# A two-layer decoder step: the last LayerNorm's mean subtracted in PSUM, its channel sums folded, some running sums added by DMA

## The chip, the core and the metric

The kernel runs on one core of a Trainium2 chip. The metric is the device time of one execution in microseconds; before the change the median of three runs is 2298.3 us (2297.39 to 2299.56). Engines are called TensorE (PE in the profile), VectorE (DVE), ScalarE (ACT), GpSimd (POOL) and SyncE (SP, which issues most DMAs). SBUF is the on-chip memory of 128 partitions, PSUM the small memory with 2 KB banks into which TensorE accumulates.

## What is computed

One step of a decoder with two layers, over 1024 prompt tokens and 8 decode tokens, model width D = 2048, all in 32-bit floats. Only the frame matters here:

```python
def layer_norm(x, g, b):                 # over the 2048 channels of a token
    mu = jnp.mean(x, -1); var = jnp.mean((x - mu)**2, -1)
    return (x - mu) * rsqrt(var + 1e-5) * g + b

z = x @ w_in                             # layer A: pooling mixer
y = (mix(z) * silu(gate)) @ w_out
h = layer_norm(ALPHA * x + y, g, b)
k, v = shared_kv(h)                      # once
z = h @ w_in                             # layer B: sliding-window attention
y = (attention(z, k, v) * silu(gate)) @ w_out
out = layer_norm(ALPHA * h + y, g, b)    # the last norm; prompt and decode tokens
```

## The kernel before

**Layout.** Channels lie on the 128 partitions, tokens along the free axis. The 2048 channels are 16 tiles of 128, kept as 8 **pairs** p = 0..7 (tiles 2p and 2p+1, side by side in one buffer). The 1032 tokens are two **chunks**: chunk 0 has 512, chunk 1 has 520 (512 and the 8 decode tokens). Chunk 1 is worked on in two **halves** of 260 tokens, `HV[0]` and `HV[1]`. A norm over channels is therefore a sum over partitions, which TensorE forms by a product with a matrix J that holds 1/2048 everywhere; J lies in `cst` as plain fp32 and in `jr` as fp32r, a form that TensorE multiplies faster with a rounded operand.

**Matmuls.** Each fp32 weight and activation is split into a rounded high part and a low part; a product is three fp32r matmuls, high x high, high x low and low x high (L594 to L596). ScalarE makes the high part (`cast`, L386), VectorE the low one (`low`, L394). The four big products, in order `ai`, `ao` (layer A, in and out) and `bi`, `bo` (layer B), use a seven-product scheme over 2x2 blocks, in three groups: A (products 0 and 5), C (1, 3, 6) and B (2, 4).

**Units and the calendar.** `plan` writes the work of TensorE out as a list of units; one unit is 25 matmuls of 260 columns, some 3 us. The clock `self.i` counts units. `on(t, f)`, `at(n, f)` and `product(n, f)` fix f at the end of a unit; `soft` puts a task with a due time into a list, from which `gentle` takes what a rough model of each engine's load allows; generators in `self.side` (the norms) are stepped when the model sees calm, or after `every` units at the latest. `in_order` then fixes the order of PE, DVE and ACT to that of the source. SP and POOL are issued in the order that the framework's own scheduler finds. SBUF is 53 slots of 1040 columns (`Mem`), each taken whole or as two half slots; a freed slot is given out again oldest first.

**The end of the kernel.** Group B of `bo` makes the output of chunk 1. Product 2 of position pos gives tiles of pair pos//2 + 4, product 4 those of pair pos//2. Positions 0 to 3 run over all 520 tokens; so pairs 4, 0, 5, 1 are finished first, in this order. Then come 16 units for positions 4 to 7, eight on the first half of the tokens and eight on the second, which finish pairs 6, 2, 7, 3. A bank for product 2 is first filled with what earlier products left (`recall`, a ScalarE copy at L716, two units ahead), and what is done is added to it in PSUM; the VectorE addition at L665 (`post`) takes product 4 out of PSUM into SBUF.

The last norm of chunk 1 goes along in pieces:
- `tail_full` is called for pairs 4, 0, 5, 1. For pair 4 it takes a rough mean by TensorE and subtracts it (`rough`, `mean`, `less`, L1187 to L1201); later units have it subtracted in PSUM (L603). For each pair it then squares (ScalarE, L1205) and adds value and square to two running sums (VectorE, `add`, L1211 and L1212, 1040 columns each).
- `tail_part` does the same for pairs 6, 2, 7 per half: `square` (L1235), `add` (L1239, L1240, 520 columns). For pair 3 it calls `tail_sums`.
- `tail_sums` (L1269) sums over partitions with plain fp32 J: running value and running square of both tiles, and value and square of pair 3, into two banks. An fp32 product stands in the trace as two instructions; over one half that is 2 banks x 4 sources x 2 = 16.
- `tail_stats` (L1281 to L1283) copies the mean, squares it, forms the variance; `rstd` (L849 to L853) makes the inverse deviation by ScalarE's reciprocal square root and one Newton step on VectorE.
- `tail_norm` for each pair: subtract the mean (`tail_less`, L1288, VectorE), multiply by the inverse deviation (L1295, VectorE, 520 columns), gain and bias for both tiles (L1299, ScalarE), and the output DMA (L1300, 260 KB). For the first half these steps run beside the units of the second half.
- `tail_end`, after the last unit, does the same for the second half, pairs in the order 4, 0, 5, 2, 1, 6, 7, 3.

The norm of chunk 0 is `ln_gen`, a generator; its two channel sums, of values and of squares, are formed one after the other by `j_gen` (L828 to L845: fold the pair, split in high and low, two matmuls with `jr`). `ao` has the same norm for its own output.

## Time and profile before

| | |
|---|---|
| median of three runs | 2298.3 us (2297.39 to 2299.56) |
| the profiled execution's own time | 2300.38 us |
| its span, first to last instruction or transfer | 2298.6 us |
| its mean granted clock of TensorE | 0.995 |
| instructions | 42483 |
| matmul instructions of TensorE | 17158 |
| `cast` L386 | 365, 1045 ns each |
| `low` L394 | 365, 1219 ns each |

How to read the rows that the prediction quotes. Engine lines of the page give busy us, share of the span and instruction count. A timeline row is: start in us from the span's start, duration (of a whole group, if several), engine, line, operation, output<-input, partitions x elements, count, and in brackets the wait just before it with the instruction that ended it. A row of waits is: engine, output, line <- releasing engine, output, line: total us, count, longest. A row of windows is: stretch, its length, then busy us and instruction count of PE, PEld, DVE, ACT and POOL, then TensorE's granted clock (1 is full speed), the DMA engines' busy share and GB/s. A row of output DMAs gives the issuing queue, the KB moved and the first and last start. "x16" is a count of instructions; "m" is a slot in SBUF, "pD" or "pO" a bank of PSUM.

### The profile page before, as it was taken

To read this page: it belongs to the slowest core of one execution; us is meant where nothing else is said; L and a number is where in the kernel's file an instruction comes from. 1 tells how busy PE (TensorE), PEld (TensorE's weight loads), DVE (VectorE), ACT (ScalarE), POOL (GpSimd) and SP (SyncE) were. 2 spreads that over 40 slices of the span, in tenths; PEclk is the share of its full clock that TensorE was granted. 3 is DMA by queue.
4 is the path that set the end of the run, shared out by engine and by line. 5 is a ranking of instruction groups with operands and counts; after the bars stand their busy time and mean duration, and the time that the engine had idled before them with its cause. 6 is when DMAs were issued, how large, how long until landed. Compare 5 with 4: busy or idle time off the path is not lost.

```text
span 2298.6 us, 42483 instructions
## 1 busy us (share of the span) xinstructions
PE 2266.7 (99%) x17158; PEld 2124.4 (92%) x17158; DVE 1577.5 (69%) x1958; ACT 1119.2 (49%) x2321; POOL 195.4 (8%) x415
## 2 busy tenths in 40 slices
PE   8999999999999999999999999999999999999996
PEld 7888999999999899998788899999999998889996
DVE  6547656746577587666786867666667778687677
ACT  5243333344334443445576644545557777443355
POOL 1101001100101011000011101010000000111000
PEclk9999999999999999999999999999999999999998
DMA  9958667673757798888497776666744566898853
GB/s 377 311 192 294 210 221 243 235 249 117 246 179 273 266 337 296 297 272 302 150 313 266 258 252 206 214 220 201 245 146 135 176 204 221 256 375 298 296 192 130
DMA packets 194645, 555.68 MB, mean 242 GB/s; under 512 B 31120, under 2 KB 36112, under 8 KB 194448
## 3 DMA queue, kind: packets, MB, share of 16 engines
q1 hardware_dynamic: 152752, 402.42, 53.9%
q0 software_dynamic: 41696, 150.55, 16.9%
q8 instruction: 134, 2.20, 0.4%
q14 instruction: 63, 0.52, 0.1%
HBM read 372.04 MB, written 171.33 MB: 236 GB/s over the span
## 4 chain that ended last, share of the span: by engine, by line
PE 92%; DVE 4%; DMA 2%; ACT 1%; issue 1%; SPq 0%; ACTq 0%; DVEq 0%
PE pD L594 27%; PE pD L595 27%; PE pD L596 27%; PE pD L1056 4%; PE pO L1574 2%; PE pS L1492 2%; PE pS L1545 1%; DMA m<-in_wob 1%; DVE m L1295 0%; DMA to<-m 0%; DVE m L1288 0%; DMA m<-to 0%; DVE m L394 0%; DVE m L926 0%; PE pD L1269 0%
## 5 line engine op out<-in xcount | busy, mean ns | idle before, releaser
L594 PE MATMUL pD<-m,m 128*128 128x260 f32 (+1 forms) x4800 | 1456.2, 303 | 9.4 <-ACT m L1836 5.8
L595 PE MATMUL pD<-m,m 128*128 128x260 f32 (+1 forms) x4800 | 1447.5, 302 | 0.2 <-DVE m L527 0.2
L596 PE MATMUL pD<-m,m 128*128 128x260 f32 (+1 forms) x4800 | 1447.6, 302 | 0.0
L594 PEld LDWEIGHTS pD<-m,m 128*128 128x128 f32 x4800 | 905.3, 189 | 52.4 <-ACT m L1836 5.8
L595 PEld LDWEIGHTS pD<-m,m 128*128 128x128 f32 x4800 | 905.2, 189 | 36.3 <-DVE m L527 1.2
L596 PEld LDWEIGHTS pD<-m,m 128*128 128x128 f32 x4800 | 904.8, 189 | 35.6
L394 DVE TENSOR_TENSOR m<-m,m 128x1024 fp32r<-128x1024 f32 x365 | 443.5, 1219 | 166.1 <-ACT m L386 148.1
L386 ACT CAST m<-m 128x1024 fp32r<-128x1024 f32 x365 | 380.1, 1045 | 40.7 <-PE pD L595 9.6
L430 DVE TENSOR_TENSOR m<-m,m 128x1024 f32<-128x1024 f32 x200 | 244.0, 1220 | 21.6 <-DMA m<-in_woa 6.0
L654 ACT COPY m<-pD 128x260 f32<-128x260 f32 (+1 forms) x126 | 55.9, 444 | 313.4 <-PE pD L596 297.0
L527 DVE TENSOR_TENSOR m<-m,m 128x1040 fp32r<-128x1040 f32 x111 | 133.6, 1235 | 21.3 <-ACT m L521 21.1
L521 ACT CAST m<-m 128x1040 fp32r<-128x1040 f32 x111 | 114.0, 1061 | 33.6 <-DMA m<-h 9.1
L663 ACT ACTIVATE m<-pD 128x260 f32<-128x260 f32 x100 | 38.6, 386 | 180.5 <-PE pD L596 167.2
L665 DVE TENSOR_TENSOR m<-pD,m 128x260 f32<-128x260 f32 x100 | 42.5, 425 | 109.8 <-PE pD L596 103.4
L1527 ACT ACTIVATE m<-m,sm 128x128 f32<-128x128 f32 x256 | 99.3, 393 | 0.0
L1056 PE MATMUL pD<-m,m 128*128 128x260 f32 (+1 forms) x576 | 91.4, 319 | 0.0
L1056 PEld LDWEIGHTS pD<-m,m 128*128 128x128 f32 x576 | 82.0, 188 | 8.3
L1557 DVE TENSOR_TENSOR m<-m,cst 128x1024 f32<-128x1024 f32 x32 | 39.1, 1222 | 73.1 <-ACT m L1553 73.1
L1540 ACT ACTIVATE m<-m,sm 128x128 f32<-128x128 f32 x256 | 81.8, 395 | 9.6 <-DVE sm L1535 9.6
L620 ACT ACTIVATE m<-pD 128x512 f32<-128x512 f32 x50 | 29.8, 596 | 115.8 <-PE pD L596 107.4
L635 ACT COPY m<-pD 128x260 f32<-128x260 f32 x68 | 25.6, 376 | 122.1 <-PE pD L596 122.1
L633 ACT ACTIVATE m<-pD 128x260 f32<-128x260 f32 x68 | 26.4, 388 | 113.5 <-PE pD L596 113.5
(183 smaller groups left out, 1689.6 us busy)
## 6 DMA issues: line engine op xcount, KB each, us to landing
m<-in_wib SPq DMA_DIRECT2D x96, 512.0 KB, 5.3
m<-in_wia SPq DMA_DIRECT2D x95, 512.0 KB, 5.5
m<-in_woa SPq DMA_DIRECT2D x48, 512.0 KB, 6.7
m<-in_wob SPq DMA_DIRECT2D x48, 512.0 KB, 6.9
sbi<-m POOLq DMA_DIRECT2D x36, 512.0 KB, 4.4
m<-sbi SPq DMA_DIRECT2D x36, 512.0 KB, 4.2
m<-in_x SPq DMA_DIRECT2D x35, 520.0 KB, 8.5
sai<-m POOLq DMA_DIRECT2D x32, 512.0 KB, 4.1
```

The costliest lines, as they stand in the source:

```text
L386: self.nc.scalar.copy(e["hi"].r[:, :1024], e["raw"].a[:, :1024])
L394: self.nc.vector.tensor_sub(o.r[:, :1024], s.a[:, :1024], e["hi"].a[:, :1024])
L430: self.nc.vector.tensor_add(s[o].a[:, :1024], s[a].a[:, :1024], s[b].a[:, :1024])
L521: self.nc.scalar.copy(h.r[:, : 2 * TMAX], s.a[:, : 2 * TMAX])
L527: self.nc.vector.tensor_sub(o.r[:, : 2 * TMAX], s.a[:, : 2 * TMAX], h.a[:, : 2 * TMAX])
L594: nc.tensor.matmul(ps[:, :w], wh[:, s], h, start=new and n2 == 0, stop=False, skip_group_check=on)
L595: nc.tensor.matmul(ps[:, :w], wh[:, s], l, start=False, stop=False, skip_group_check=on)
L596: nc.tensor.matmul(ps[:, :w], wl[:, s], h, start=False, stop=n2 == 7, skip_group_check=on)
L654: self.evac(ph, pos)(self.dest(ph, pos, m, 0)(cs), ps[:, : cs.stop - cs.start])
L1056: nc.tensor.matmul(ps[:, : cs.stop - cs.start], ws[:, s], d[:, cs], start=f0 and k == 0, stop=l0 and k == 3,)
L1527: nc.scalar.activation(x["s3"][:, i, :], x["s3"][:, i, :], AF.Exp, bias=nm[:, i : i + 1], scale=0.125, accum_out=rs[:, i : i + 1],)
L1540: nc.scalar.activation(x["s3"][:, i, :], x["s3"][:, i, :], AF.Copy, scale=rs[:, i : i + 1])
```

## The change

What it does, part by part.
- **Two sums at once.** A new `two_gen` takes the place of `j_gen` in the norms of chunk 0: values and squares are folded, split and multiplied with `jr` side by side, into two banks. `ln_gen` yields once more at odd pairs in the last norm, and that norm's pace is set to 1 at unit 7 of the group where it was 2 at unit 13.
- **Casts.** A lone weight's cast may be queued at `min(L_CAST + 2, lead - 2)` units ahead of use; where the load leads by less than the usual 11 units, this is later than before.
- **Running sums.** In `tail_full`, pairs 5 and 1 are added to the running sums by accumulating DMAs on GpSimd's queue (`accum_op=add`, SBUF to SBUF), squares and additions right at the end of the unit. In `tail_part` the same holds for pair 6 (both halves) and pair 2 (first half). The other additions stay on VectorE, one unit earlier but for pair 2 in the second half.
- **Folded sums.** After pair 7, VectorE adds tile 1 of both running sums to tile 0. Pair 3 is folded in too (tile 0 of the second half and both tiles of the first). `tail_sums` then has one source for each bank, and in the second half also the last tile of pair 3.
- **First half earlier.** Its sums stay where they were, statistics and norms come one unit earlier, and the norm of its pair 3 moves into `tail_end`.
- **Mean in PSUM.** The new `tail_end` handles six of eight pairs so: TensorE copies a tile into a bank with the identity matrix in fp32 (`fill`), adds `jr` times the high and low part of -16 x mean (`less`; 128 rows of 1/2048 sum to 1/16), and VectorE multiplies the bank by the inverse deviation. Pairs 4 and 0 keep the subtraction on VectorE. Three tiles of the twelve get gain and bias on VectorE, the others on ScalarE; results go to SBUF or back into the bank.

```diff
         self.on(t - lead, load, 6)
-        self.rounds(t, e)
+        self.rounds(t, e, min(L_CAST + 2, lead - 2))
         return e
...
-    def rounds(self, t, e):
+    def rounds(self, t, e, early=L_CAST + 2):
...
-        e["queue"] = lambda: self.soft("a", t - L_CAST - 2, t - L_CAST + 1, cast_task)
+        e["queue"] = lambda: self.soft("a", t - early, t - L_CAST + 1, cast_task)
...
+    def two_gen(self, T, acc, sq, mu, q, v):
+
+        nc, w = self.nc, []
+        for s in (acc, sq):
+            t = self.pair_view(s, T)
+            nc.vector.tensor_add(t[:, 0], t[:, 0], t[:, 1])
+            e = self.mem.full()
+            w.append((s, t, e, e.r[:, :T], e.r[:, TMAX : TMAX + T]))
+            nc.scalar.copy(w[-1][3], t[:, 0])
+        yield
+        for s, t, e, hi, lo in w:
+            nc.vector.tensor_sub(lo, t[:, 0], hi.bitcast(F32))
+            s.free()
+        yield
+        ps = []
+        for s, t, e, hi, lo in w:
+            ps.append(self.psW()[:, :T])
+            for i, a in enumerate((hi, lo)):
+                nc.tensor.matmul(ps[-1], self.jr, a, start=i == 0, stop=i == 1)
+            e.free()
+        yield
+        nc.scalar.activation(q, ps[0], AF.Square)
+        nc.scalar.copy(mu, ps[0])
+        nc.vector.scalar_tensor_tensor(v, ps[1], EPS, q, op0=ALU.add, op1=ALU.subtract)
+        yield
...
-        yield from self.j_gen(T, acc, lambda s, ps: nc.scalar.copy(mu[:, s], ps))
-        w = self.mem.full()
-        q, v = w.a[:, :T], w.a[:, TMAX : TMAX + T]
         if c == 0:
-            sq = self.l_sq
-            nc.vector.tensor_mul(q, mu, mu)
+            w = self.mem.full()
+            q, v = w.a[:, :T], w.a[:, TMAX : TMAX + T]
+            yield from self.two_gen(T, acc, self.l_sq, mu, q, v)
         else:
+            yield from self.j_gen(T, acc, lambda s, ps: nc.scalar.copy(mu[:, s], ps))
+            w = self.mem.full()
+            q, v = w.a[:, :T], w.a[:, TMAX : TMAX + T]
...
-        yield from self.j_gen(
-            T, sq,
-            lambda s, ps: nc.vector.scalar_tensor_tensor(v[:, s], ps, EPS, q[:, s], op0=ALU.add, op1=ALU.subtract)
-            if c == 0 else nc.vector.tensor_scalar(v[:, s], ps, EPS, None, op0=ALU.add),
-        )
+            yield from self.j_gen(T, sq, lambda s, ps: nc.vector.tensor_scalar(v[:, s], ps, EPS, None, op0=ALU.add))
...
                 if c == 0:
                     nc.vector.tensor_sub(t, t, b2(mu))
+                    if name is None and p % 2:
+                        yield
                 nc.vector.tensor_mul(t, t, b2(rr))
...
             a = self.tacc
-            nc.vector.tensor_add(flat(a), flat(self.tp[4] if q == 0 else a), flat(s))
-            nc.vector.tensor_add(flat(self.tq[4]), flat(self.tq[4]), flat(self.tq[q]))
-            self.tq.pop(q).free()
+            z = self.tq.pop(q)
+            if q == 0:
+                nc.vector.tensor_add(flat(a), flat(self.tp[4]), flat(s))
+                nc.vector.tensor_add(flat(self.tq[4]), flat(self.tq[4]), flat(z))
+                z.free()
+                return
+            nc.gpsimd.dma_start(flat(a), flat(s), accum_op=ALU.add)
+            nc.gpsimd.dma_start(flat(self.tq[4]), flat(z), accum_op=ALU.add)
+            z.free(True)
...
-        for n, go in ((3, square), (4, add)):
+        for n, go in ((3, square), (4, add)) if q in (0, 4) else ((0, square), (0, add)):
             self.at(n, go)
...
+        a, z = self.pair_view(self.tacc, TMAX), self.qv(4)
+
         def add():
-            a, z = self.pair_view(self.tacc, TMAX), self.qv(4)
+            y = self.tq.pop((q, h.start))
+            if q == 6 or q == 2 and not final:
+                nc.gpsimd.dma_start(a[:, :, h], self.tv(q)[:, :, h], accum_op=ALU.add)
+                nc.gpsimd.dma_start(z[:, :, h], y.v(2, THM), accum_op=ALU.add)
+                y.free(True)
+                return
             nc.vector.tensor_add(a[:, :, h], a[:, :, h], self.tv(q)[:, :, h])
-            nc.vector.tensor_add(z[:, :, h], z[:, :, h], self.tq[q, h.start].v(2, THM))
-            self.tq.pop((q, h.start)).free()
-
-        if q == 3 and final:
+            nc.vector.tensor_add(z[:, :, h], z[:, :, h], y.v(2, THM))
+            y.free()
+            if q == 7:
+                for u in (a, z):
+                    nc.vector.tensor_add(u[:, 0, h], u[:, 0, h], u[:, 1, h])
+
+        def fold():
+            nc.vector.tensor_add(a[:, 0, h], a[:, 0, h], self.tv(q)[:, j, h])
+            nc.vector.tensor_add(z[:, 0, h], z[:, 0, h], self.tq[q, h.start].v(2, THM)[:, j])
+
+        if q == 3:
             square(j)
-            self.product(0 if j else 1, lambda: self.tail_sums(h, (j,), j == 0, j == 1), 1)
+            if j and final:
+                self.product(0, lambda: self.tail_sums(h, (1,)), 1)
+                return
+            self.at(0, fold, 6)
+            if j:
+                self.product(1, lambda: self.tail_sums(h, ()), 1)
+                self.at(1, lambda: self.tail_stats(h))
+                for n, p in zip((2, 3, 3, 4, 4, 5, 6), (4, 0, 5, 1, 6, 2, 7)):
+                    self.at(n, lambda p=p: self.tail_norm(p, h))
             return
         if j == 0:
             return
         self.at(0, square)
-        if q != 3:
-            self.at(1, add)
-            return
-        self.product(1, lambda: self.tail_sums(h, (0, 1), True, True), 1)
-        self.at(2, lambda: self.tail_stats(h))
-        for n, p in zip((3, 4, 4, 5, 5, 6, 6, 7), (4, 0, 5, 1, 6, 2, 7, 3)):
-            self.at(n, lambda p=p: self.tail_norm(p, h))
-
-    def tail_sums(self, h, js, first, stop):
+        self.at(1 if q == 2 and final else 0, add, 6)
+
+    def tail_sums(self, h, js):
         J = self.cst[:, K_J : K_J + P]
-        if first:
-            self.R[h.start] = self.psW(), self.psW()
-        for ps, a, z in zip(
-            self.R[h.start], (self.pair_view(self.tacc, TMAX), self.qv(4)),
+        R = self.R[h.start] = self.psW(), self.psW()
+        pairs = list(zip(
+            R, (self.pair_view(self.tacc, TMAX), self.qv(4)),
             (self.tv(3)[:, :, h], self.tq[3, h.start].v(2, THM)),
-        ):
-            srcs = ([a[:, j, h] for j in range(2)] if first else []) + [z[:, j] for j in js]
-            for i, v in enumerate(srcs):
-                self.nc.tensor.matmul(
-                    ps[:, :THM], J, v, start=first and i == 0, stop=stop and i == len(srcs) - 1,
-                    skip_group_check=not (first and stop),
-                )
+        ))
+        for n, j in enumerate((None,) + js):
+            for ps, a, z in pairs:
+                v = a[:, 0, h] if j is None else z[:, j]
+                self.nc.tensor.matmul(ps[:, :THM], J, v, start=n == 0, stop=n == len(js), skip_group_check=True)
...
     def tail_end(self):
-        h = HV[1]
-        self.tail_stats(h, lambda: [self.tail_less(p, h) for p in (4, 0)])
-        for p in (4, 0, 5, 2, 1, 6, 7, 3):
-            self.tail_norm(p, h, p not in (4, 0))
-
+
+        nc, h = self.nc, HV[1]
+        ident = self.cst[:, K_ID : K_ID + P]
+        mb, vb = (b[:, :THM] for b in self.R[h.start])
+        _, r, qq, v = (self.L[k][:, h] for k in "mrqv")
+        sl = self.mem.full()
+        hi, lo = (sl.r[:, i * THM : (i + 1) * THM] for i in range(2))
+        mean = mb[:, None, :].to_broadcast([P, 2, THM])
+        banks = [self.psO(), self.psD(), self.psD(), self.psD(), self.psW(), self.psW()]
+        plain, tiles = (4, 0), [2 * p + j for p in (5, 1, 2, 6, 7, 3) for j in range(2)]
+        done = []
+
+        def z(k):
+            return self.tv(k // 2)[:, k % 2, h]
+
+        def bank(n):
+            if n >= 6:
+                banks.append((self.psO, self.psD, self.psD, self.psD, self.psW, self.psW)[n % 6]())
+            return banks[n][:, :THM]
+
+        def fill(n):
+            nc.tensor.matmul(bank(n), ident, z(tiles[n]), start=True, stop=False, skip_group_check=True)
+
+        def less(n):
+            for i, t in enumerate((hi, lo)):
+                nc.tensor.matmul(banks[n][:, :THM], self.jr, t, start=False, stop=i == 1, skip_group_check=True)
+
+        def scale(k, src, eng):
+            g, b = (self.prm[:, i + k : i + k + 1] for i in (C_GB, C_BB))
+            if eng == "a":
+                nc.scalar.activation(z(k), src, AF.Identity, bias=b, scale=g)
+            else:
+                nc.vector.tensor_scalar(z(k), src, g, b, op0=ALU.mult, op1=ALU.add)
+            done.append(k)
+            if k ^ 1 in done:
+                p = k // 2
+                nc.sync.dma_start(self.io["y1"][:, 2 * p : 2 * p + 2, h], self.tv(p)[:, :, h])
+
+        self.tail_norm(3, HV[0])
+        nc.scalar.activation(qq, mb, AF.Square)
+        nc.scalar.mul(hi, mb, -16.0)
+        nc.vector.scalar_tensor_tensor(v, vb, EPS, qq, op0=ALU.add, op1=ALU.subtract)
+        nc.vector.scalar_tensor_tensor(lo, mb, -16.0, hi.bitcast(F32), op0=ALU.mult, op1=ALU.subtract)
+
+        def between():
+            for p in plain[:1]:
+                t = self.tv(p)[:, :, h]
+                nc.vector.tensor_sub(t, t, mean)
+
+        for n in range(4):
+            fill(n)
+        for n in range(4, 6):
+            less(n - 4)
+            fill(n)
+        less(2)
+        less(3)
+        self.rstd(v, r, qq, between)
+        two = r[:, None, :].to_broadcast([P, 2, THM])
+        for n, k in enumerate(tiles):
+            if n in (1, 4):
+                p = plain[n > 1]
+                t = self.tv(p)[:, :, h]
+                if n > 1:
+                    nc.vector.tensor_sub(t, t, mean)
+                nc.vector.tensor_mul(t, t, two)
+                for j in range(2):
+                    scale(2 * p + j, t[:, j], "a")
+            if n + 4 < len(tiles):
+                less(n + 4)
+            b = banks[n][:, :THM]
+            eng = "v" if n in (7, 9, 11) else "a"
+            o = z(k) if eng == "v" or n + 6 < len(tiles) else b
+            nc.vector.tensor_mul(o, b, r)
+            scale(k, o, eng)
+            if n + 6 < len(tiles):
+                fill(n + 6)
...
-        self.on(f["bo", "B"] + 13, pace(2))
+        self.on(f["bo", "B"] + 7, pace(1))
```

More of the change, by code (lines that the diff above doesn't have):

```diff
@@ L476, in weights @@
                 src = {0: a11, 5: a12, 2: ws[:, 0, :], 4: ws[:, 1, :]}[u.idx]
-                held[k] = self.lone(u.t, src, L_LOAD - (4 if u.keep else 2 if (u.ph, u.grp) == ("bi", "B") else 0))
+                lead = L_LOAD - (4 if u.keep else 2 if (u.ph, u.grp) == ("bi", "B") else 0)
+                held[k] = self.lone(u.t, src, lead)
             u.ent = held[k]
```

## The prediction

> **What bounds the kernel now.** I read the page first, then the waits of TensorE over the whole span, then the timelines of TensorE, VectorE and ScalarE from 2195 us on, where every part of the change that is not a reordering lies.
>
> ```profile
> span 2298.6 us, 42483 instructions
> PE 2266.7 (99%) x17158; PEld 2124.4 (92%) x17158; DVE 1577.5 (69%) x1958; ACT 1119.2 (49%) x2321; POOL 195.4 (8%) x415
> PE 92%; DVE 4%; DMA 2%; ACT 1%; issue 1%; SPq 0%; ACTq 0%; DVEq 0%
> PE pS L1492 <- DVE m L1475: 2.3, 1, 2.3
> PE pD L594 <- DVE m L629: 2.2, 1, 2.2
> PE pD L594 <- ACT m L663: 0.3, 1, 0.3
> PE pD L1269 <- DVE m L1239: 0.5, 1, 0.5
> ```
>
> TensorE is busy 99% of the span, and its waits between the first matmul and the last are a few microseconds in all. So two things count: what TensorE itself has to do, and how long the kernel runs on after the last matmul unit. The next rows are TensorE's timeline at the two places where channel sums are taken.
>
> ```profile
> 2252.29 3.67 PE L1269 MATMUL pD<-m,cst 128*128 128x260 f32 x16
> 2255.60 0.47 PE L594 MATMUL pD<-m,m 128*128 128x260 f32 x1
> 2276.52 0.28 PE L603 MATMUL pD<-m,jr 128*128 128x260 f32 x1
> 2277.34 3.77 PE L1269 MATMUL pD<-m,cst 128*128 128x260 f32 x16 [0.54 <-DVE m L1239]
> ```
>
> The sums of the first half of the tokens stand in TensorE's queue between two units and hold it for 2255.60 - 2252.29 = 3.31 us, 0.207 for each of 16 instructions. The last unit ends at 2276.52 + 0.28 = 2276.80; I call this moment E. From E to the end of the span are 21.8 us, and this stage belongs to VectorE, as its timeline and ScalarE's show.
>
> ```profile
> 2274.91 0.42 DVE L665 TENSOR_TENSOR m<-pD,m 128x260 f32<-128x260 f32 x1
> 2275.25 0.69 DVE L1288 TENSOR_TENSOR m<-m,m 128x520 f32<-128x520 f32 x1
> 2275.97 0.70 DVE L1295 TENSOR_TENSOR m<-m,m 128x520 f32<-128x520 f32 x1
> 2276.59 0.69 DVE L1239 TENSOR_TENSOR m<-m,m 128x520 f32<-128x520 f32 x1
> 2277.81 0.42 DVE L665 TENSOR_TENSOR m<-pD,m 128x260 f32<-128x260 f32 x1
> 2281.12 0.43 DVE L1282 TENSOR_TENSOR m<-m 128x260 f32<-128x260 f32 x1 [2.89 <-ACT m L1281]
> 2281.65 0.43 DVE L1283 SCALAR_TENSOR_TENSOR m<-pD,m 128x260 f32<-128x260 f32 x1
> 2283.67 0.43 DVE L852 SCALAR_TENSOR_TENSOR m<-m 128x260 f32<-128x260 f32 x1
> 2284.13 0.43 DVE L853 SCALAR_TENSOR_TENSOR m<-m,m 128x260 f32<-128x260 f32 x1
> 2284.59 1.31 DVE L1295 TENSOR_TENSOR m<-m,m 128x520 f32<-128x520 f32 x2
> 2293.27 0.70 DVE L1295 TENSOR_TENSOR m<-m,m 128x520 f32<-128x520 f32 x1
> 2280.71 0.38 ACT L1281 COPY m<-pD 128x260 f32<-128x260 f32 x1 [2.02 <-PE pD L1269]
> 2282.11 0.42 ACT L849 ACTIVATE m<-m 128x260 f32<-128x260 f32 x1 [1.03 <-DVE m L1283]
> 2285.33 3.08 ACT L1299 ACTIVATE m<-m,prm 128x260 f32<-128x260 f32 x6 [2.79 <-DVE m L1295]
> 2294.06 1.10 ACT L1299 ACTIVATE m<-m,prm 128x260 f32<-128x260 f32 x2 [0.31 <-DVE m L1295]
> L1300 SPq DMA_DIRECT2D out_y<-m x8: 372/372/373, 2286.5 to 2295.2; - x8
> DMA to landing us min/median/max: 2.2/2.2/2.2
> ```
>
> The steps I take from these rows are starts apart. An operation of 260 columns follows an independent one after 0.34 us and one that it depends on after 0.46; of 520 columns, after 0.61 and 0.72. ScalarE starts 0.79 after the 520-wide operation that feeds it, and one of its gain-and-bias operations costs 3.08 / 6 = 0.51. After E: the first multiply by the inverse deviation comes at E + 7.79, the eight pairs go through VectorE, the last output is issued at 2295.2 = E + 18.4, lands 2.2 later at 2297.4, and 1.2 us after that the span ends.
>
> **The change, part by part.** First half, channel sums folded. VectorE now adds the two halves of a pair before TensorE sums, so 4 instructions stand where 16 stood: 4 x 0.207 = 0.83 us in place of 3.31. Nothing else can use TensorE's queue there, so **2.48 us** are saved outright. The folds (six VectorE operations of 260 columns, about 0.4 us each) lie under a unit of 3 us, if their sources are there in time (below).
>
> E to the first multiply. The new queue of VectorE after E, by the order in which the changed program issues: the last evacuation at E + 0.04, subtract and multiply of pair 3 of the first half (they were moved here) at 0.38 and 1.10. ScalarE, in order, does that pair's two gain-and-bias operations from 1.10 + 0.79 = 1.89 on, and only then, at 2.92, the new square of the mean; this is the wait the move adds. The eight remaining sum instructions of TensorE end by about E + 1.8, ahead of it. The variance follows the square by 0.41 (as L1282 follows L1281), at 3.33; the low part of the mean at 3.68; one subtract at 4.03, done with at 4.65, by when the root (0.46 after the variance, 0.42 long) is ready; then three dependent steps of 0.46. The first multiply stands at E + 6.03 in place of E + 7.79: **1.76 us** saved.
>
> The loop. Six of eight pairs lose their subtract on VectorE: their 12 tiles are multiplied straight out of PSUM, 12 x 0.34 = 4.08, the price of L665, which also reads PSUM. Two pairs stay: 0.61 for one, 0.72 + 0.61 for the other. Three tiles get gain and bias on VectorE too, priced as L852 for want of a nearer row: 3 x 0.11 more for the dependence, 2 x 0.35, and 0.42 for the last. The sum is 7.47, so the last output can be issued at E + 13.56 and not E + 18.4: with the 1.76, 4.84 in all, **3.08 us** of it in the loop. ScalarE has 13 gain-and-bias operations left, 6.6 us, and ends just before; TensorE has eight pairs of subtracting matmuls (0.12 each, a unit's 25 take 3 us) and six fills of 0.41, 4.4 us. Both fit, ScalarE barely. Writes of VectorE to PSUM occur nowhere before; I price them between 0.34 and twice that (three of them, +1.0 at worst, and below 0.34 has no ground).
>
> Outputs. Eight of 260 KB now come within some 6 us.
>
> ```profile
> 2288.00:2290.00 2.00, 0.00 (x0) 0.00 (x0) 1.97 (x4) 1.53 (x4) 0.00 (x0) 0.50 0.76 269
> 2042.00:2044.00 2.00, 1.64 (x7) 1.65 (x8) 2.00 (x3) 1.02 (x2) 0.00 (x0) 0.53 1.03 414
> 2042.36 0.59 PE L594 MATMUL pD<-m,m 128*128 128x260 f32 x1 [2.15 <-DVE m L629]
> ```
>
> At a share of 0.76 the outputs moved 269 GB/s, so 354 at full share, 0.75 us for each. The last four become ready within 1.8 us and queue: I add **0.45 us**.
>
> The accumulating DMAs. Four running additions over the whole width and four of the first half leave VectorE (about 4 x 1.14 + 4 x 0.61 = 7 us of it, beside TensorE's units, so worth nothing by themselves); two more go in the second half, with 4 us to spare. No DMA of this trace adds. They are chained on POOL's queue, each waiting for the one before on the same sum, and there is a second link: the squares of pairs 6, 2 and 7 of the first half are written to one and the same half slot, so ScalarE's square for pair 2 waits until the addition of pair 6 has landed, and the square for pair 7 until that of pair 2 has. Behind it in ScalarE's order stands the copy that seeds the bank of the unit starting at about 2249.5, and TensorE waits for that one.
>
> ```profile
> 2226.30 0.42 DVE L665 TENSOR_TENSOR m<-pD,m 128x260 f32<-128x260 f32 x1
> 2228.24 1.06 ACT L1205 ACTIVATE m<-m 128x1040 f32<-128x1040 f32 x1
> 2239.95 0.42 DVE L665 TENSOR_TENSOR m<-pD,m 128x260 f32<-128x260 f32 x1
> 2240.46 0.64 ACT L1235 ACTIVATE m<-m 128x520 f32<-128x520 f32 x1 [1.60 <-DVE m L665]
> ```
>
> Pair 1 is evacuated at 2226.3; its square can be added from 2226.3 + 0.45 + 1.06 = 2227.8 on. If a whole-width addition takes T and a half-width one U, pair 6 lands at 2227.8 + T + U; the square of pair 2 can start at 2240.5 anyway, and takes 0.64; then U, and 3.3 us of square, add, two folds, evacuation, square and copy. TensorE waits for max(0, U - 5.1 + max(0, T + U - 12.7)). The nearest rows are plain stores from POOL's queue, of 260 KB (L621) and 520 KB (L646), and, in this very stretch, 512 KB loads (L371):
>
> ```profile
> DMA to landing us min/median/max: 2.3/5.4/9.1
> DMA to landing us min/median/max: 2.9/6.3/9.2
> DMA to landing us min/median/max: 3.7/4.5/5.3
> ```
>
> I take U = 4.5 and T = 6, near the loads of the same stretch: no wait. At the lower ends there is none either, and nothing to gain; at the upper ends 9.1 - 5.1 + 18.3 - 12.7 = 9.6 us. The Trainium skill, "Collectives: The Full Stack", section "The bandwidth ceiling: the fold count and why AG ≠ RS ≠ AR", says that an add in the DMA path costs two source reads and so half the rate; no run here shows it yet, and by it the chain would lie nearer the upper ends.
>
> Two sums at once in the norm of the first chunk, and casts queued a unit or two later for weights loaded late: the same matmuls in another place, orders on VectorE and ScalarE shifted by a few places, all beside TensorE. I cost them at nothing. Each of the two waits of 2.3 and 2.2 us above could go or come once more, so plus or minus 2 us is the bound.
>
> Sum: 2.48 + 1.76 + 3.08 - 0.45 = 6.9 us off a span of 2298.6, so 2291.7. The profiled execution itself took 2300.38, 1.8 us around its span, and lies 2.1 above the median of 2298.3; taken off the median, the forecast is **2291.4 us**.
>
> **Rivals.** (1) The additions land late. For: the chain has four links, ScalarE and POOL wait in order, and the DMA queues carry loads of the next norm at the same time. Against: loads in this stretch land in 4.5 us. It gives 2291.4 plus the wait; with T = 7.5 and U = 6.5, 2.7 us, 2294.1. (2) The same mechanism past its point of decision, on the other side: once T and U both pass about 8.3 us the wait, 3.2 + 3.9 = 7.1, has eaten the gain. At the upper ends of the rows it is 9.6 us and the time 2301.0; with both at twice the stores' medians, 12.6 and 10.8, as an addition that has to read its destination too might take, it is 5.7 + 10.7 = 16.4 us and the time **2307.8**. (3) The tail doesn't shrink as worked out, because TensorE, now needed in it, runs at half clock. The window row at 2042 shows a granted clock of 0.53 after a gap of 2.15 us. After E I count no gap over 0.8 us. At half clock from E + 4.1 on, the subtracting matmuls and fills take 0.48 and 0.83 each, 12 and 8 of them left, some 12.4 us to E + 16.5, VectorE ends 1 us later, and the time is 2291.4 + 3.9 = 2295.3. The Trainium skill, "TensorE: Matmul & The Clock Gate", section "What's actually happening", has the clock fall only after an idle window of about 3.4 us; the gap of 2.15 us here is shorter, so the trace speaks for an earlier fall than the page. (4) Outputs, not VectorE, end the kernel: at the 1.34 us per pair of before they would end near 2296; against it, all eight landed in 2.2 us, so nothing queued.
>
> **How the numbers follow.** Forecast, with 2289.8 to 2293.0 as its own range: 0.60. Additions late but short of break-even: 0.18, of which 0.05 still over 0.2% faster. Past it: 0.12, of which 0.10 over 0.2% slower. Half clock or outputs: 0.05 each. A difference of 0.2%, 4.6 us, is about what a measurement of this kernel can tell from no change, so faster means under 2293.7: 0.60 + 0.05 = 0.65; slower means over 2302.9, 0.10; the rest, 0.25, is within. The range runs from 2288.8 (the forecast with one of the earlier waits gone) to 2301.0, the upper ends of the stores' rows, which takes in rivals 1, 3 and 4 and the near part of 2; some 0.12 lies above it and a little below.
>
> **What would show it.** In the changed profile: the sum instructions between the two units 4 in place of 16, and the next unit 0.8 us after them; no TensorE wait over 0.5 us between 2235 and 2255; additions landing in 3 to 6 us; ScalarE's square of the mean some 2.9 us after the last unit, the first multiply at 6.0, the last output issued at 13.6, the span ending 17.4 after it. A wait of TensorE on ScalarE's seed copy near 2249, or a granted clock near 0.5 before the last tile, would make it wrong.

## The result and the profile after: slower, by additions that land late

The changed kernel takes 2307.54 us (median of six runs, 2305.26 to 2309.04) against 2299.29 before (six runs): a ratio of 1.0033, with a 95% interval of 1.0022 to 1.0044. The forecast was 2291.4 with a range to 2301.0; the time lies above it, where the prediction's second rival had put 2307.8. The profiled execution took 2309.04 us, with a span of 2307.3.

The page shows TensorE with 28 more instructions than before and 6.6 us more busy time, and says little else. The waits of TensorE from 2200 us on say where the time is:

```profile
span 2307.3 us, 42566 instructions
PE 2273.3 (99%) x17186; PEld 2129.6 (92%) x17186; DVE 1569.2 (68%) x1959; ACT 1118.3 (48%) x2322; POOL 206.0 (9%) x425
PE pD L595 <- ACT m L664: 9.7, 1, 9.7
PE pD L595 <- ACT pD L717: 2.3, 1, 2.3
```

Before, the same stretch had waits of 0.3 and 0.5 us. L664 is ScalarE's evacuation of a bank and L717 its seed copy; so the question is what held ScalarE. Its timeline names the releaser in brackets:

```profile
2251.77 0.64 ACT L1267 ACTIVATE m<-m 128x520 f32<-128x520 f32 x1 [12.26 <-DMA m<-m]
2252.31 0.37 ACT L664 ACTIVATE m<-pD 128x260 f32<-128x260 f32 x1
2259.99 0.64 ACT L1267 ACTIVATE m<-m 128x520 f32<-128x520 f32 x1 [5.62 <-DMA m<-m]
2262.79 0.37 ACT L717 COPY pD<-m 128x260 f32<-128x260 f32 x1
```

L1267 is the square of pair 2 and then of pair 7, first half. Both wait for a DMA from SBUF to SBUF, the accumulating ones. GpSimd's timeline shows when these were issued (L1243 and L1244: value and square of pairs 5 and 1, whole width; L1274 and L1275: value and square of pairs 6 and 2, half width):

```profile
2220.46 0.90 POOL L1243 DMA_DIRECT2D m<-m  x1 [35.62 <-DVE m L950]
2221.54 0.87 POOL L1244 DMA_DIRECT2D m<-m  x1 [0.19 <-issue]
2227.45 0.85 POOL L1243 DMA_DIRECT2D m<-m  x1 [5.04 <-DVE m L666]
2230.20 0.83 POOL L1244 DMA_DIRECT2D m<-m  x1 [1.90 <-DMA m<-m]
2239.66 1.20 POOL L1274 DMA_DIRECT2D m<-m  x1 [8.63 <-ACT pD L717]
2247.89 1.18 POOL L1275 DMA_DIRECT2D m<-m  x1 [7.03 <-DMA m<-m]
2252.01 1.19 POOL L1274 DMA_DIRECT2D m<-m  x1 [2.94 <-DMA m<-m]
2256.10 1.19 POOL L1275 DMA_DIRECT2D m<-m  x1 [2.90 <-issue]
```

and these, in the same order of lines, how long they took to land:

```profile
DMA to landing us min/median/max: 6.4/8.9/11.5
DMA to landing us min/median/max: 8.0/10.0/12.1
DMA to landing us min/median/max: 3.8/3.8/7.9
DMA to landing us min/median/max: 3.8/3.8/4.3
```

Pair 1's square was issued at 2230.2 and landed 12.1 us later, at 2242.3. Pair 6's square was issued only at 2247.89, which is 0.3 us after pair 6's value had landed (2239.66 + 7.9), though it adds to another buffer. It landed at 2251.7, and ScalarE started pair 2's square at 2251.77. For pair 2 the same again: the second addition 4.1 us behind the first, landing near 2259.9, ScalarE at 2259.99. (Ahead of this last issue the profile names no releaser, only "issue"; the time fits the landing of the first, 2252.01 + 3.8, as at pair 6.)

Each of the two waits of TensorE costs more than its length. Its timeline and the granted clock (the last column but two) behind the two waits:

```profile
2252.74 0.59 PE L595 MATMUL pD<-m,m 128*128 128x260 f32 x1 [9.74 <-ACT m L664]
2263.22 0.39 PE L595 MATMUL pD<-m,m 128*128 128x260 f32 x1 [2.29 <-ACT pD L717]
2267.84 1.04 PE L1317 MATMUL pD<-m,cst 128*128 128x260 f32 x4
2268.53 0.48 PE L595 MATMUL pD<-m,m 128*128 128x260 f32 x1
2289.57 0.28 PE L604 MATMUL pD<-m,jr 128*128 128x260 f32 x1
2252.00:2256.00 4.00, 3.26 (x15) 3.27 (x16) 0.11 (x1) 2.36 (x5) 1.19 (x1) 0.50 0.64 142
2263.00:2268.00 5.00, 4.78 (x26) 4.79 (x27) 1.55 (x4) 0.86 (x3) 0.00 (x0) 0.66 0.24 97
```

The three units of this stretch end 25.0 us after the unit ahead of them and took 9.6 before: 15.4 us lost, 11.7 of them waits (12.0 against 0.3) and 3.7 half clock. The last unit ends at 2289.57 + 0.28 = 2289.85, which is E here, against 2276.80.

The gains are there as well, and nearly as priced. The sums of the first half (L1317) hold TensorE for 2268.53 - 2267.84 = 0.69 us where they held it for 3.31. After E:

```profile
2292.70 0.36 ACT L1387 ACTIVATE m<-pD 128x260 f32<-128x260 f32 x1
2295.84 0.43 DVE L1420 TENSOR_TENSOR m<-pO,m 128x260 f32<-128x260 f32 x1
L1384 SPq DMA_DIRECT2D out_y<-m x8: 372/373/433, 2298.0 to 2303.3; - x8
```

ScalarE's square of the mean at E + 2.85, the first multiply at E + 5.99, the last output issued at E + 13.5, the span's end at E + 17.45. In sum: +15.4 for the stretch with the waits, -2.6 for the sums, -4.35 after E, and +0.2 elsewhere make 8.7, the difference of the spans.

### The profile page after: what moved, and what is told of

The parts are those of the page before. It is cut to its first block, busy times and chain, and to the rows that moved or that the text cites. A ratio compares the mean times of both kernels' runs of the same rounds, so it can differ in the third digit from the quotient of the medians.

```text
span 2307.3 us, 42566 instructions
## 1 busy us (share of the span) xinstructions
PE 2273.3 (99%) x17186; PEld 2129.6 (92%) x17186; DVE 1569.2 (68%) x1959; ACT 1118.3 (48%) x2322; POOL 206.0 (9%) x425
## 4 chain that ended last, share of the span: by engine, by line
PE 89%; DVE 4%; DMA 4%; ACT 1%; issue 1%; SPq 0%; DVEq 0%; ACTq 0%; POOLq 0%
PE pD L595 27%; PE pD L596 26%; PE pD L597 26%; PE pD L1082 4%; PE pO L1690 2%; PE pS L1608 2%; DMA m<-m 1%; PE pS L1661 1%; DVE m L528 1%; DMA m<-in_wob 1%; DVE m L394 1%; DMA to<-m 0%; DMA m<-to 0%; DMA m<-in_wkv 0%; DMA m<-in_x 0%
## 5 line engine op out<-in xcount | busy, mean ns | idle before, releaser
L664 ACT ACTIVATE m<-pD 128x260 f32<-128x260 f32 x100 | 38.5, 385 | 175.3 <-PE pD L597 167.0
```

## Experiments

The theory to be tested (A): the additions land late and hold TensorE through ScalarE; everything else was priced right. Its rivals: the moved work and VectorE's load cost something too; or the reuse of one half slot, and not the chain, is at fault.

**The additions back on VectorE.**

```diff
-            nc.gpsimd.dma_start(flat(a), flat(s), accum_op=ALU.add)
-            nc.gpsimd.dma_start(flat(self.tq[4]), flat(z), accum_op=ALU.add)
-            z.free(True)
+            nc.vector.tensor_add(flat(a), flat(self.tp[4] if q == 0 else a), flat(s))
+            nc.vector.tensor_add(flat(self.tq[4]), flat(self.tq[4]), flat(z))
+            z.free()
...
-            if q == 6 or q == 2 and not final:
-                nc.gpsimd.dma_start(a[:, :, h], self.tv(q)[:, :, h], accum_op=ALU.add)
-                nc.gpsimd.dma_start(z[:, :, h], y.v(2, THM), accum_op=ALU.add)
...
```

> The changed kernel with its ten accumulating DMAs (six additions of a pair's values and squares: four transfers of the whole width, six of half width) put back on VectorE at the old places; folds, subtraction in PSUM, two sums at once, cast times stay. Theory A (the additions land late and hold TensorE through ScalarE's square, all else was priced right): TensorE's waits of 9.7 and 2.3 us and the two units at half clock behind them (3.7 us) go, 2307.5 - 15.4 = 2292.1 us, range 2290.5 to 2293.5. Rival B (the reordering, casts or two sums cost something too): over 2294. Rival C (VectorE, with some 7 us more in its queue, binds TensorE in place of the DMAs): over 2294 with TensorE waits on VectorE between 2225 and 2255.

Measured: 2296.9 us (before 2299.27), ratio 0.9988 (0.9979 to 0.9997). The long waits are gone, and 10.6 of the 15.4 us are back. But the time is 4.8 us above theory A. The waits, what ScalarE's evacuation waited for, and VectorE's stage, here and in the kernel before, say where most of it is:

```profile
PE pD L595 <- ACT m L664: 2.8, 2, 2.3
2244.28 0.39 ACT L664 ACTIVATE m<-pD 128x260 f32<-128x260 f32 x1 [1.66 <-DVE m L1239]
2224.00:2252.00 28.00, 25.48 (x198) 25.06 (x197) 27.81 (x33) 17.49 (x27) 0.00 (x0) 0.94 0.43 157
2224.00:2252.00 28.00, 27.68 (x231) 27.47 (x230) 27.62 (x31) 15.93 (x27) 0.00 (x0) 1.00 0.59 187
```

VectorE is busy 27.81 of 28 us. In the kernel before (last row) it was 27.62 there, so it had no room either. Its late addition of pair 1's squares (L1239) holds ScalarE's evacuation, which holds TensorE for 2.3 us, with some 1.5 us of half clock behind. Rival C holds in this form: TensorE waits on ScalarE, and ScalarE on VectorE. The remaining 1 us is not explained.

**The additions alone, on the kernel before.** The edit is the reverse of the first, with the squares and additions at the changed kernel's places.

> The kernel of before with nothing changed but the ten accumulating DMAs and the places of their squares and additions. Theory A: the loss of 15.4 us without the gains, 2299.3 + 15.4 = 2314.7 us, range 2311 to 2319. Rival B (the loss comes out of the whole change, in its order and slots): below 2306.

Measured: 2312.45 us, ratio 1.0055 (1.0041 to 1.0069), 13.2 us slower and within theory A's range. The DMAs do the damage without the rest of the change.

**A slot for each square.**

```diff
-                self.tq[q, h.start] = self.mem.half()
+                self.tq[q, h.start] = self.mem.half() if final or q == 3 else self.mem.full()
```

> The changed kernel, but the squares of pairs 6, 2 and 7 of the first half each get a slot of their own, so that ScalarE waits for no landing. If the reused half slot is the whole cause: TensorE's waits go, 2292 us. If the chain of landings itself is late (theory A): VectorE's addition of pair 7 waits for pair 2 to land, near 2255 in place of about 2247, and holds the evacuations behind it; TensorE's wait shrinks from 12 to about 6 us and stands on VectorE, 2300 us, range 2296 to 2304.

Measured: 2307.62 us, ratio 1.0037 (1.0024 to 1.0051): nothing gained, and the number was missed by 7.6 us. The wait moved:

```profile
2241.93 1.04 ACT L386 CAST m<-m 128x1024 fp32r<-128x1024 f32 x1 [6.96 <-DMA m<-m]
2258.70 0.70 DVE L1279 TENSOR_TENSOR m<-m,m 128x520 f32<-128x520 f32 x1 [4.11 <-DMA m<-m]
```

A weight's cast now got a slot from which an addition was still reading, and VectorE's addition of pair 7 waited for pair 2's landing. So the half slot is only where the lateness showed; taken away there, it shows elsewhere.

**Copies in place of additions.** `accum_op=ALU.add` is struck out in all ten places.

> The changed kernel, its ten DMAs writing in place of adding (same bytes, same order and waits; the running sums are left out, so its norm is not the reference's). If a transfer that adds moves at half the rate of one that copies (173 GB/s against 342 GB/s, by the shares of the two kinds of queue in the changed kernel's last 93 us), the landings fall from 8.9 and 10.0 us to 5 or 6 for the whole width and from 3.8 to about 3 for half, TensorE's wait to 1 to 3 us, and the time to 2294, range 2292 to 2298. If the rate is not the cause and the links in the chain are: over 2303.

Measured: 2293.7 us, ratio 0.9969 (0.9960 to 0.9978); the one TensorE wait left in the stretch is 0.6 us. The first rows are of pair 6's additions in the second half of the changed kernel: GpSimd's queue over 9.5 us with nothing else on it (packets, MB, share of 16 engines), and a window in which the first of the two moves alone (the last two columns are the DMA share and GB/s). Then the same two rows for the same transfers as copies, GpSimd's issues for pair 2, and the landings, in the order of lines of above as far as L1274:

```profile
q0 software_dynamic: 544, 0.53, 37.9%
2274.50:2275.90 1.40, 1.40 (x15) 1.40 (x14) 1.01 (x2) 0.48 (x2) 0.00 (x0) 1.00 1.16 172
q0 software_dynamic: 160, 0.53, 15.7%
2260.10:2260.80 0.70, 0.70 (x9) 0.70 (x8) 0.00 (x0) 0.70 (x3) 0.00 (x0) 1.00 1.02 368
2243.66 0.71 POOL L1274 DMA_DIRECT2D m<-m  x1 [3.10 <-DMA m<-m]
2244.43 0.72 POOL L1275 DMA_DIRECT2D m<-m  x1
DMA to landing us min/median/max: 6.3/7.0/7.6
DMA to landing us min/median/max: 6.5/7.9/9.2
DMA to landing us min/median/max: 2.5/2.5/4.5
```

While it has the DMA engines to itself, the addition moves 172 GB/s and the copy 368, a factor of 2.1. (The queue rows' shares, 37.9% against 15.7%, would say 2.4. But the addition alone has a share of 1.16; above 1 the times of packets overlap, so a rate cannot be read from its share.) The additions also take 272 packets for one transfer and not 80, and two copies are issued 0.8 us apart, without waiting for a landing. The whole-width copies landed later than the expected 5 to 6 us, in company with loads and stores, and still were no harm.

**Only the whole width by DMA.** Pairs 6 and 2 are put back on VectorE, as in the first experiment.

> The changed kernel with only the four transfers of the whole width (pairs 5 and 1) as accumulating DMAs; pairs 6 and 2 are added by VectorE, each one unit after it is done. If the landings of the whole width (8.9 and 10.0 us in the changed kernel, 6.4 to 12.1) are enough to lose the gain: VectorE's addition of pair 6 waits some 5 us for pair 1, evacuations stand behind it, TensorE loses 3 to 5 us and some 1.5 of half clock, 2297 to 2302 us, most likely 2299. If the loss comes from the half-width ones alone: about 2293.

Measured: 2300.12 us (before 2300.9 in these runs), ratio 1.0000 (0.9991 to 1.0009). As expected, now VectorE stands and waits, at pair 6's two additions:

```profile
2238.81 0.70 DVE L1273 TENSOR_TENSOR m<-m,m 128x520 f32<-128x520 f32 x1 [4.31 <-DMA m<-m]
2242.16 0.70 DVE L1274 TENSOR_TENSOR m<-m,m 128x520 f32<-128x520 f32 x1 [2.65 <-DMA m<-m]
```

and TensorE waits 6.2 us, more than the expected 3 to 5, for what is queued behind. The whole-width landings alone are enough to lose the gain.

**Half-width additions by tile.**

```diff
-                nc.gpsimd.dma_start(a[:, :, h], self.tv(q)[:, :, h], accum_op=ALU.add)
-                nc.gpsimd.dma_start(z[:, :, h], y.v(2, THM), accum_op=ALU.add)
+                for u in range(2):
+                    nc.gpsimd.dma_start(a[:, u, h], self.tv(q)[:, u, h], accum_op=ALU.add)
+                for u in range(2):
+                    nc.gpsimd.dma_start(z[:, u, h], y.v(2, THM)[:, u], accum_op=ALU.add)
```

> The changed kernel with each half-width addition issued as two DMAs of one tile (128 rows of 260) in place of one of two tiles (256 pieces). In the changed kernel GpSimd issues the second half-width addition 0.3 us after the first has landed, 4.1 us after it was issued, though it adds to another buffer; the whole-width ones (128 pieces) and the copies of half width follow one another without that. Theory D (the number of pieces of an adding DMA makes GpSimd wait until the one before is done): now values and squares are issued back to back, pair 6's squares land about 5 us earlier and each later link is 3 us shorter; TensorE's wait falls from 12 to about 5 us, 2299 us, range 2296 to 2303. Rival E (GpSimd waits for something else, such as a semaphore or any two additions under way): unchanged, 2306 to 2309, or worse for the additional issues of some 0.85 us each.

Measured: 2301.02 us (before 2300.9), ratio 1.0003 (0.9993 to 1.0012), against 1.0033 for the changed kernel; TensorE's longest wait is 7.1 us and not 9.7. GpSimd's issues for pair 6 (L1275 value, L1277 square):

```profile
2237.70 1.72 POOL L1275 DMA_DIRECT2D m<-m  x2 [8.60 <-ACT pD L717]
2241.12 0.85 POOL L1277 DMA_DIRECT2D m<-m  x1 [1.71 <-issue]
2244.99 0.84 POOL L1277 DMA_DIRECT2D m<-m  x1 [3.02 <-DMA m<-m]
```

The two value additions of 128 pieces go out back to back, as pair 5's two whole-width ones (128 pieces too) do in the changed kernel; the fourth waits for a landing again. So how the additions are cut matters, and the time lies in theory D's range. What GpSimd waits for inside stays open. A limit on the pieces of additions under way would fit as well as theory D: the changed kernel issued pair 6's value (256 pieces) at 2239.66 while pair 1's square (128) was under way until 2242.3, so 384 were let through, and each issue that would have made it 512 was held, the fourth one above included. No run here separates the two.

**What the moved work is worth.** All additions on VectorE, and the first chunk's norm, its pace and the casts as before.

> All additions on VectorE, and the parts that only move work undone as well: the norm of the first chunk as before (one sum after the other, its old pace), casts at their old times. What is left of the change is the folded sums, the earlier first half and the mean subtracted in PSUM. With the additions alone put back on VectorE, TensorE still lost 2.3 us on ScalarE and half a unit to half clock, since VectorE was never idle from 2224 to 2252 us. Theory: that came from the norm's quicker pace beside the additions on VectorE; now no wait over 0.5 us there, and 2299.3 - 6.9 = 2292.4 us, range 2290.5 to 2294. Rival: the folds and the earlier additions of pair 7 crowd VectorE by themselves: a TensorE wait over 1 us between 2235 and 2255, and 2295 to 2297.

Measured: 2297.26 us, ratio 0.9993 (0.9984 to 1.0002), missed by 5 us. The early stretch is clean (no wait over 0.6 us until 2270), but now the second half stalls; the last row is the kernel before:

```profile
2272.12 0.39 PE L595 MATMUL pD<-m,m 128*128 128x260 f32 x1 [2.51 <-ACT m L664]
2262.00:2278.00 16.00, 12.95 (x94) 12.53 (x93) 14.25 (x23) 11.41 (x23) 0.00 (x0) 0.89 0.51 183
2262.00:2278.00 16.00, 15.46 (x128) 15.20 (x127) 15.69 (x28) 11.95 (x25) 0.00 (x0) 1.00 0.43 151
```

With the old pace a part of the first chunk's norm is left for the stretch in which the first half's norm runs, and that starts a unit earlier than before. VectorE has no gap from 2256 to 2274, and the evacuation stands in ScalarE's order behind gain-and-bias operations that waited 2.51 us for VectorE, until 2268.83. Before, VectorE was busy 15.69 of these 16 us without the folds. The quick pace only moves the crowd from here to the stretch around 2244.

**Pair 5 alone by DMA, old pace.** The additions of q = 5 stay on GpSimd, right behind its unit; the rest as in the experiment before.

> As the one before, but the additions of pair 5, and these alone, by accumulating DMA: the earliest of the chain, with some 20 us until VectorE adds pair 1 to the same sums. If the DMA additions do harm only where their landing is waited for: no new wait, VectorE is rid of 2.3 us, and the time is that of the version before, within 1 us (2291.5 to 2293.5). If an accumulating DMA costs by itself, by its traffic: over 2294.

Measured: 2297.03 us, ratio 0.9984 (0.9976 to 0.9993). No wait for the landing, as expected, but the late wait (2.3 us, near 2271) stays. The median is that of the version before within 0.3 us, as one reading had it; the expected figure was missed with that version's, since VectorE was relieved in the wrong stretch.

**Pair 5 alone by DMA, quick pace.** The changed kernel, with only q = 5 left on GpSimd.

> The changed kernel (its quick norm of the first chunk kept) with the additions of pair 5 alone by accumulating DMA, all others on VectorE. Reading so far: with all on VectorE, TensorE lost 2.3 us at 2244 and 1.5 to half clock, since VectorE was never idle from 2224 to 2252; with the old pace it lost 2.5 us at 2272 instead, as VectorE is full there. If VectorE's load is what binds, the 2.3 us of pair 5's additions, taken from VectorE just ahead of 2235, remove the wait at 2244: 3.8 us under the version with all on VectorE, a ratio to before of 0.9972 or 6.5 us less than before, range 5 to 7.5 us less. If not the load but the order on ScalarE holds TensorE: the wait stays, 2 to 3 us less than before.

Measured: 2293.37 us (before 2299.39), ratio 0.9968 (0.9956 to 0.9981): faster than both kernels, and hit. The waits from 2200 on, VectorE's stage, and the landings of pair 5, which nobody waits for:

```profile
PE pD L595 <- ACT pD L717: 0.9, 1, 0.9
PE pD L595 <- ACT m L664: 0.8, 2, 0.4
2224.00:2252.00 28.00, 26.69 (x221) 26.27 (x220) 26.26 (x34) 17.00 (x28) 0.00 (x0) 1.00 0.56 190
DMA to landing us min/median/max: 8.9/8.9/8.9
DMA to landing us min/median/max: 11.6/11.6/11.6
```

VectorE is down to 26.26 of 28 us, which is enough.

**Pair 6 of the second half by DMA too.**

> As the one before, and pair 6 of the second half by accumulating DMA too (its landing, 8 us after it is issued for the two, is wanted by VectorE some 9 us later). VectorE is rid of 1.2 us where it is full as well. If a landing with slack costs nothing: the same time within 0.7 us, and the wait of 0.4 us that the version with all on VectorE showed near 2272 goes. If VectorE's next addition (pair 2) waits for the landing: a new TensorE wait between 2268 and 2285, 1 to 4 us slower.

Measured: 2294.92 us, ratio 0.9979 (0.9970 to 0.9988). In the profile the wait of 0.4 us near 2268 goes, no new one comes, and the span is 2291.9 against 2292.3. The median is 1.55 us higher, more than the 0.7 us expected, but the two intervals overlap; which of the two versions is faster is not settled.

**The subtraction in PSUM undone**, on the version with pair 5 alone:

```diff
...
+        self.tail_norm(3, HV[0])
+        self.tail_stats(h, lambda: [self.tail_less(p, h) for p in (4, 0)])
+        for p in (4, 0, 5, 2, 1, 6, 7, 3):
+            self.tail_norm(p, h, p not in (4, 0))
```

> As the first of these three, with the subtraction of the mean in PSUM undone: after the last unit the norm of the second half as before (VectorE subtracts for all eight pairs; pair 3 of the first half stays behind the last unit). By the prediction's terms: the first multiply some 0.9 us later, the loop 3.1 us longer, 0.45 less of queueing outputs: 3.5 us slower than with it, range 3 to 4.5; from the end of the last unit to the end of the span 21 us in place of 17.45. If the subtraction in PSUM gives nothing: the same time.

Measured: 2299.68 us, ratio 0.9997 (0.9989 to 1.0006). From E to the end of the span are 20.7 us, against 17.45 in the version it is made from: 3.2 of the expected 3.5. The medians differ by 6.3. In the profiled executions the spans differ by 5.6, and the 2.4 us of it that do not lie behind E are there by 2242 already. 1.7 of them come from far ahead of the edit, where both run the same program, as the granted clock of one stretch shows (first with the subtraction in PSUM, then without):

```profile
1950.00:1960.00 10.00, 10.00 (x77) 8.71 (x77) 4.71 (x8) 5.09 (x13) 0.10 (x1) 1.00 0.78 272
1950.00:1960.00 10.00, 10.00 (x58) 8.48 (x58) 3.60 (x7) 3.98 (x11) 0.00 (x0) 0.83 0.76 252
```

At a clock of 0.83 ten microseconds lose 1.7. The kernel before has this half-clock period in its profile as well, and so has the version with pair 6 of the second half by DMA, which runs the same program up to there; so the edit at the end does not decide it. What makes up the rest of the difference between the medians stays open.

## Why the prediction was wrong, step by step

- **Accumulating DMAs: the step that failed.** The prediction took U = 4.5 and T = 6, "near the loads of the same stretch: no wait". For the transfers that mattered, pair 1's, T was 11.5 and 12.1, twice the figure taken. As copies the same two took 7.6 and 9.2, so a part is the traffic of the stretch, and a part that an addition moves 172 GB/s where a copy moves 368. The Trainium skill's rule of two source reads ("Collectives: The Full Stack", "The bandwidth ceiling: the fold count and why AG ≠ RS ≠ AR"), stated there for a collective's reduce, stood in the prediction as the argument against the change; the trace agrees with it, at a factor of 2.1. The prediction named the rule and then took a copy's duration.
- **A wait that no step had.** U by itself was 3.8, under the figure taken (7.9 for pair 6's value, beside pair 1's square). But the model let value and square of a pair fly side by side, and GpSimd issued the second only when the first had landed: 5.6 us at pair 6 (2242.3, when pair 1's square had landed, to 2247.89), near 3 more at pair 2. Nor did the model let pair 1's square wait until pair 5's had landed, 2.4 us. In sum, pair 6's additions were to land at 2227.8 + 6 + 4.5 = 2238.3 and the last landed at 2251.7, which is 2227.8 + 2.4 + 12.1 + 5.6 + 3.8. The experiment by tile got 6.9 of the 15.4 us back (1.0033 against 1.0003, times 2299).
- **Half clock behind the waits**: 3.7 us that the prediction counted for the tail (its third rival) and not for its first two. In the tail it did not come: from E on the granted clock was 1.00.
- **The second rival** named the place (the reused half slot, ScalarE's square, the seed copy) and came out at 2307.8. Of the 12.0 us of waits 2.3 stood on the seed copy and 9.7 on an evacuation behind the square. That the number is right is luck, two errors that cancel: its U of 10.8 stood for a U of 3.8 with a wait ahead of it and for the half clock. Its T of 12.6 was near the 12.1 measured; at a chance of 0.12 it still had little weight.
- **"Worth nothing by themselves"**, of the VectorE time that the DMAs free, also failed: with all additions back on VectorE 4.8 us of the gain are missing. VectorE is busy 27.6 of 28 and 15.7 of 16 us in two stretches of the kernel before; the average of 69% hid that.
- **Folded sums**: 2.62 us measured (3.31 - 0.69), 2.48 predicted. Right.
- **E to the first multiply**: 5.99 measured, 6.03 predicted. Right, with the wait behind pair 3's gain and bias where it was put (E + 2.85; 2.9 predicted).
- **Loop and outputs**: last output at E + 13.5, end at E + 17.45; 13.56 (its own terms add up to 13.50) and 17.4 predicted. Undoing the subtraction costs 3.2 us behind E in the profiled executions; the 6.3 us between those medians are not explained by it.
- **Two sums, casts, pace "at nothing"**: not shown to be right as a size, and wrong in kind. They move VectorE's crowd from one stretch to another, and which of the two stalls depends on them. With all additions on VectorE they are worth some 1 us (0.9993 against 0.9988), with pair 5 by DMA some 3.7 us (0.9984 against 0.9968); the intervals overlap in both cases.
- The sum of 6.9 us was reached, but by the version with only pair 5 on the DMA: 6.0 us between medians, 7.4 by the ratio.

## What to carry to other kernels

Work moved from an engine to a DMA is free only where its landing has slack; walk the chain of landings with a transfer that adds at about half a copy's rate, and ask who stands in order behind the one that waits. An engine's load has to be read per stretch: one that is busy 69% on average can be full exactly where the change adds or removes work. When one term of a change has a rule against it and no row for it, let the estimate take the rule's side.

## What the runs showed of the hardware

- An adding DMA of 260 KB in 256 pieces: 272 packets, 172 GB/s with the DMA engines to itself, 3.8 us to land; as a copy 80 packets, 368 GB/s, 2.5 us. GpSimd takes 1.19 us to issue it, against 0.71 for the copy.
- Behind an adding DMA of 256 pieces GpSimd issued the next one only when the first had landed, in all three pairs of the changed kernel, some 0.3 us after the landing. Pair 2's two copies of the same shape followed each other after 0.8 us, and pair 5's two adding ones of 128 pieces after 1.1 us.
- From 2200 us on, waits of TensorE of 2.3 us and more were each followed by half clock in these profiles (some 1.5 us lost behind those of 2.3 to 2.5 us), and those of 1.2 us and less were not. The length of a wait alone does not decide it: in the changed kernel's profile the waits of 2.31 us before 2043.32 and of 2.32 us before 1920.19 had a granted clock of 1.00 behind them. The waits of 2.3 to 2.5 us are shorter than the idle window of about 3.4 us that the Trainium skill, "TensorE: Matmul & The Clock Gate", "What's actually happening", gives.
